# Moving one row sum (S.1) later in VectorE's order, and three last stores to other issuers, in a convolution with max pooling

## The chip, the cores and the metric

The kernel runs on one core of a Trainium2 chip. The metric is the time of one execution on the device, in microseconds, lower is better. Five engines work side by side, each through its own list of instructions in order: TensorE (PE in the profile, its weight loads PEld), VectorE (DVE), ScalarE (ACT), GpSimd (POOL) and SyncE (SP). SP issues DMA transfers only; ScalarE and GpSimd can issue them too.

## The reference

```python
x_pad = np.pad(x, ((0, 0), (0, 0), (1, 1), (1, 1)))            # x: 16 x 64 x 64 x 64, f32
for kh in range(3):
    for kw in range(3):                                        # weight: 128 x 64 x 3 x 3
        conv[b, co] += weight[co, ci, kh, kw] * x_pad[b, ci, kh:kh+64, kw:kw+64]
output[b, c, i, j] = np.max(conv[b, c, 2*i:2*i+2, 2*j:2*j+2])  # 16 x 128 x 32 x 32
```

## The kernel before

Two images lie on the 128 partitions, 64 channels each; `h` (0 or 1) is the image of the pair. The pictures are cut into quarters of 16 rows, that is 8 pooled rows, so that one product of TensorE is 64 channels by 8 rows by 64 columns and fills one of the eight PSUM banks (`acc[:, bank]`). There are 32 such units, handled in two ways. A K unit reads a bf16 copy of its rows (`kx`) and takes five products; a W unit reads f32 rows (`wx`), forms four sums of rows and takes four products. Write r0 and r1 for the two picture rows of a pooled row, r-1 and r2 for their neighbours, G0, G1, G2 for the three rows of the filter. Both kinds split the two convolved rows into a part that they share and a part of each. The maximum of the two separate parts is taken first (VectorE), TensorE then adds the shared part into the same bank, and the maximum over neighbouring columns follows.

A text, `ORDER`, holds every step of the kernel in one sequence written out by hand; each engine gets its own steps in that sequence, and semaphores between engines follow from the data. A step is a name, the unit's number and, for most, the image:

- `E.i` (VectorE) or `e.i` (GpSimd): r1 - r0 of W unit i. `S.i` (VectorE): r0 + r1 of W unit i. `Z.i` and `Y.i` (GpSimd): r-1 - r1 and r2 - r0. `KS.i` (VectorE): r0 + r1 of K unit i. All are line 260, and their tiles are called we, ws, wz, wy and ks.
- `P...` (TensorE, line 202): products, two of them joined by a plus sign and interleaved, three matmuls each (one per filter column). P2, P0, P3 and P1 of a W unit read we, wz, wy and ws; PAa, PAb, PBa and PBb of a K unit read kx, PR reads ks. P1 and PR add the shared part. A number after a colon is the bank.
- `EV`/`ev` (ScalarE, line 290): one bank copied to SBUF; `SE` (ScalarE, line 295): minus one bank into another; `MX`/`mx` (VectorE, line 299): the maximum of a bank and a copied one, written back into the bank; `OD`/`od` (ScalarE, line 303): the odd columns copied out; `CM`/`cm` (VectorE, line 327): the maximum of even and odd columns into the output tile `o`. Capitals are K units, small letters W units.
- `X...`: casts of the first K unit's rows to bf16. `LD.i`: load of a W unit's rows, issued by SP. `L<n>`: load of two K units' rows, issued by GpSimd with a cast on the way.

Two rules outside `ORDER` bear on the change. The first is an order edge: every sum that GpSimd makes waits for the VectorE step with two SBUF operands (E, S, KS and the like) that stands last before it in `ORDER`:

```python
def on_vector(inst):
    sbuf_op[0] = inst
    return inst

def on_gpsimd(inst):
    behind(inst, sbuf_op[0])
    return inst
```

The second is the way in which the last stores are issued. `act_left` counts the ScalarE steps that are still to come in `ORDER`. The outputs of the last two units are stored image by image; a store that comes up while `act_left` is 1 or 0 goes into a list, `late`, and is issued once `act_left` is 0, the first from that list by ScalarE, the second by SyncE, and so on in turn. All others are issued by SyncE at once.

The last steps of `ORDER` that matter to this are `CM.12.1 od.18.0 cm.18.0 OD.12.0 CM.12.0 od.18.1 cm.18.1`.

Of the kernel before, what the change touches and what calls it, by code (L numbers as in the profile page):

```python
# [10 lines left out]
def kernel(  # L11
# [274 lines left out]
    ev, od, ot = {}, {}, {}  # L286
# [19 lines left out]
    act_left = [0]  # L306
# [2 lines left out]

    def store_late(dst, src):  # L310
        late.append((dst, src))
        if act_left[0] <= 1:
            flush_late()

    def flush_late():
        while late and act_left[0] == 0:
            stored["late"] = stored.get("late", 0) + 1
            queue = nc.scalar if stored["late"] % 2 else nc.sync
            dst, src = late.pop(0)
            queue.dma_start(out=dst, in_=src)  # L320

    def colmax(c, i, h):
        g = (c, i, h)
        if (c, i) not in ot:
            ot[c, i] = o_pool.tile([128, 2, R, WO], FP32, name="o")
        o = ot[c, i]
        nc.vector.tensor_tensor(  # L327
            out=o[:, h],
            in0=acc[:, tb[g], :, 0::2],
            in1=od.pop(g),  # L330
            op=MAX,
        )
        free.add(tb.pop(g))
        p, q = place[c, i]
        dst = out[2 * p : 2 * p + 2, :, q * R : (q + 1) * R, :].rearrange("b c h w -> c b (h w)")
        src = o.rearrange("p b h w -> p b (h w)")
        stored[c, i] = stored.get((c, i), 0) + 1
        if order_of.index((c, i)) >= len(order_of) - 2:
            if act_left[0] <= 1:
                store_late(dst[:, h], src[:, h])  # L340
            else:
                nc.sync.dma_start(out=dst[:, h], in_=src[:, h])
        elif stored[c, i] == 2:
            nc.sync.dma_start(out=dst, in_=src)
# [72 lines left out]
    for name, f in ("ev", evac), ("mx", rowmax), ("od", odd), ("cm", colmax):  # L417
        steps[name] = lambda i, h, f=f: f("w", i, h)
        steps[name.upper()] = lambda i, h, f=f: f("k", i, h)
# [7 lines left out]
        PAx.0.0:6+PAx.0.1:7 GM/V PAa.0.0+PAa.0.1 VD0/A VG1/V LD.1 PAb.0.0+PAb.0.1 XE/V VG2/A TGM:2 KS.0  # L427
        TGP:4 E.0 VGM/A PBa.0.0:0+PBa.0.1:1 EV.0.0 Z.0 VGP/V LD.2 PBb.0.0+PBb.0.1 EV.0.1 MX.0.0
        P2.0.0:4+P2.0.1:3 X1/A S.0 X1b/A L0 PAy.1.0:7+PAy.1.1:2 PAa.1.0+PAa.1.1 SE.0.1:5 MX.0.1 Y.0 SE.0.0:6
        PAb.1.0+PAb.1.1 X2/A E.1 PR.0.0+P0.0.1 EV.1.0 P0.0.0+PR.0.1 EV.1.1 S.1 LD.3 ev.0.1 PBa.1.0:7+P3.0.1 KS.1 Z.1 OD.0.1  # L430
        P2.1.0:2+PBa.1.1:3 OD.0.0 CM.0.1 ev.0.0 mx.0.1 P3.0.0+PBb.1.1 SE.1.0:4 Y.1 PBb.1.0+P2.1.1:1 MX.1.1
        P0.1.0+P1.0.1 CM.0.0 e.2 MX.1.0 SE.1.1:0 P3.1.0+PR.1.1 LD.4 mx.0.0 ev.1.0 PR.1.0+P0.1.1 Y.2 LD.5
        OD.1.1 mx.1.0 od.0.1 P1.0.0+P3.1.1 OD.1.0 CM.1.1 ev.1.1 P1.1.0+P2.2.1:2 cm.0.1 Z.2 od.0.0 mx.1.1
        PAa.2.0:5+PAa.2.1:3 SE.2.1:1 CM.1.0 PAb.2.0+PAb.2.1 L1 od.1.0 cm.0.0 KS.3 PBa.2.0:7+PBa.2.1:6 EV.2.1
        E.3 LD.6 PBb.2.0+P0.2.1 EV.2.0 S.2 LD.7 P2.2.0:3+P1.1.1 KS.2 ev.2.1 Z.3 cm.1.0 PAa.3.0:5+PBb.2.1
# [117 lines left out]
```

## Time and profile before

| | us |
|---|---|
| median of 3 runs | 105.14 (104.82 to 105.29) |
| the profiled execution, its own time | 105.48 |
| its span in the profile | 103.6 |
| TensorE busy | 97.3 (94% of the span) |
| VectorE busy | 89.2 (86%) |
| ScalarE busy | 81.9 (79%) |
| GpSimd busy | 67.1 (65%) |
| 16 DMA engines, mean rate | 220 GB/s |

The granted TensorE clock of the profiled execution was 0.995 of full speed. The profiled execution is 0.34 us above the median, and 1.88 us of its time lie outside the span. In the views below, an instruction's line gives its start in us from the start of the span, how long it took (or how long a merged group of instructions took in all), engine, line, operation, output and inputs, and in brackets the idle time of the engine before it with the event that ended the idle time. A TensorE weight load overlaps matmuls, and an engine may start an instruction some hundredths of a microsecond before the end of the one before it.

### The profile page before, as it was taken

The page shows a single profiled execution, that of the slowest core. Times are in us where ns is not written, and L with a number is a line of the kernel's source. Part 1 is how long each engine was busy: PE and PEld are TensorE (multiplying, and loading weights), DVE is VectorE, ACT ScalarE, POOL GpSimd, SP SyncE. Part 2 cuts the span into 40 slices and gives each one's busy share as a digit, 9 for nine tenths or more (in the row PEclk, how much of TensorE's full clock was granted, in tenths as well). Part 3 has the DMA queues.
Part 4 walks back from the last instruction along what each step waited for, and adds up shares of the span by engine and source line. Part 5 has one row for each costly group of instructions (what it writes and reads, how often), then busy time and mean ns, then how long its engine had stood idle before and what let it go on. Part 6 is the DMA issues. An engine that isn't in the chain of part 4 may idle for free.

```text
span 103.6 us, 2522 instructions
## 1 busy us (share of the span) xinstructions
PE 97.3 (94%) x894; PEld 53.4 (52%) x894; DVE 89.2 (86%) x178; ACT 81.9 (79%) x178; POOL 67.1 (65%) x76
## 2 busy tenths in 40 slices
PE   6899998999999999999999999999999999999920
PEld 2365434555665555555555755555555555666600
DVE  1697598999698999987988999989999999989960
ACT  4579966887897867799879988889889988988640
POOL 7306559947959687976895946892993598590000
PEclk9999999999999999999999999999999999999997
DMA  2987988899999997589989988999956841512352
GB/s 59 354 284 224 234 196 286 237 300 165 284 382 320 161 212 291 192 201 206 218 195 327 357 224 264 299 218 222 378 190 139 197 173 41 196 70 76 131 210 96
DMA packets 13069, 22.81 MB, mean 220 GB/s; under 512 B 1024, under 2 KB 9216, under 8 KB 13056
## 3 DMA queue, kind: packets, MB, share of 16 engines
q1 hardware_dynamic: 12048, 19.63, 58.0%
q0 software_dynamic: 864, 2.88, 18.8%
q8 instruction: 7, 0.11, 0.5%
q10 hardware_dynamic: 144, 0.13, 0.4%
q14 instruction: 6, 0.05, 0.2%
HBM read 17.14 MB, written 8.39 MB: 246 GB/s over the span
## 4 chain that ended last, share of the span: by engine, by line
PE 76%; DMA 8%; DVE 8%; POOL 2%; issue 2%
PE acc L202 75%; DMA wx<-in_x_dram 6%; DMA wraw<-in_weight_dram 3%; DVE acc L299 2%; DVE o L327 2%; POOL wz L260 1%; POOL wy L260 1%; DVE wq L395 1%; DVE we L260 1%; DVE ws L260 1%; DVE wq L364 0%; DVE wq L356 0%; DVE wt L180 0%; PE acc L164 0%; DVE ks L260 0%
## 5 line engine op out<-in xcount | busy, mean ns | idle before, releaser
L202 PEld LDWEIGHTS <-wt 64*128 64x128 bf16 x858 | 50.8, 94 | 41.3 <-issue 1.2
L202 PE MATMUL acc<-kx,wt 64*128 64x512 bf16 (+4 forms) x324 | 57.1, 365 | 0.0
L299 DVE TENSOR_TENSOR acc<-acc,ev 128x512 f32<-128x512 f32 x64 | 42.4, 692 | 4.1 <-PE acc L202 2.5
L290 ACT COPY ev<-acc 128x512 f32<-128x512 f32 x64 | 36.6, 592 | 6.2 <-PE acc L202 5.7
L260 POOL TENSOR_TENSOR wz<-wx 128x512 bf16<-128x512 f32 x19 | 24.1, 1273 | 10.9 <-DVE ks L260 4.6
L202 PE MATMUL acc<-wy,wt 64*128 64x504 bf16 (+1 forms) x114 | 29.6, 377 | 0.4 <-POOL wy L260 0.4
L260 POOL TENSOR_TENSOR wy<-wx 128x512 bf16<-128x512 f32 x19 | 24.1, 1272 | 8.2 <-PE acc L202 3.1
L202 PE MATMUL acc<-wz,wt 64*128 64x504 bf16 (+1 forms) x114 | 29.2, 376 | 0.2 <-POOL wz L260 0.2
L202 PE MATMUL acc<-we,wt 64*128 64x504 bf16 (+1 forms) x114 | 29.1, 377 | 0.0
L202 PE MATMUL acc<-ws,wt 64*128 64x504 bf16 (+1 forms) x114 | 29.1, 377 | 0.0
L327 DVE TENSOR_TENSOR o<-acc,od 128x256 f32<-128x256 f32 x64 | 25.2, 417 | 2.1 <-ACT od L303 1.7
L303 ACT COPY od<-acc 128x256 f32<-128x256 f32 x64 | 23.0, 380 | 4.5 <-PE acc L202 3.7
L295 ACT ACTIVATE acc<-acc 128x512 f32<-128x512 f32 x38 | 22.1, 587 | 3.8 <-DVE o L327 2.1
L202 PE MATMUL acc<-ks,wt 64*128 64x504 bf16 (+1 forms) x78 | 20.2, 377 | 0.0
L260 POOL TENSOR_TENSOR we<-wx 128x512 bf16<-128x512 f32 x11 | 14.0, 1272 | 5.1 <-PE acc L202 3.4
L260 DVE TENSOR_TENSOR ws<-wx 128x512 bf16<-128x512 f32 x19 | 13.9, 738 | 0.0
L260 DVE TENSOR_TENSOR we<-wx 128x512 bf16<-128x512 f32 x8 | 6.0, 750 | 1.1 <-DMA wx<-in_x_dram 1.1
L260 DVE TENSOR_TENSOR ks<-kx 128x512 bf16<-128x512 bf16 x13 | 5.4, 419 | 0.1
L105 POOL DMA_DIRECT2D kx<-in_x_dram x6 | 3.5, 590 | 0.0
L487 PE MATMUL acc<-const-bfloat16-1.0 128*128 128x512 bf16 x6 | 2.7, 623 | 0.8 <-PEq L534 0.8
L356 DVE TENSOR_TENSOR wq<-wraw 128x192 bf16<-128x192 f32 x1 | 0.5, 502 | 2.4 <-DMA wraw<-in_weight_dram 2.4
L164 PE MATMUL acc<-ident,wq 128*128 128x128 bf16 x28 | 2.1, 220 | 0.5 <-DVE wq L395 0.3
(28 smaller groups left out, 17.6 us busy)
## 6 DMA issues: line engine op xcount, KB each, us to landing
out_dram<-o SPq DMA_DIRECT2D x30, 256.0 KB, 4.6
wx<-in_x_dram SPq DMA_DIRECT2D x9, 512.0 KB, 7.1
wx<-in_x_dram SPq DMA_DIRECT2D x5, 480.0 KB, 6.4
wx<-in_x_dram SPq DMA_DIRECT2D x4, 544.0 KB, 6.4
kx<-in_x_dram POOLq DMA_DIRECT2D x3, 496.0 KB, 8.0
kx<-in_x_dram POOLq DMA_DIRECT2D x2, 528.0 KB, 8.9
wx<-in_x_dram SPq DMA_DIRECT2D x1, 576.0 KB, 9.9
ksecond<-in_x_dram SPq DMA_DIRECT2D x2, 256.0 KB, 4.1
```

What stands on the lines that cost most here:

```text
L105: return nc.gpsimd.dma_start(out=ktile(i)[:, lo:hi, :], in_=rows_of(p, lo, hi))
L164: nc.tensor.transpose(turned_rows(m)[:, j, :], wq[:, BLOCKS[m] - 1 + j : BLOCKS[m] + 1 + j, :].rearrange("a b c -> a (b c)"), ident,)
L202: lambda kw=kw, o0=o0, o1=o1, c0=c0, c1=c1: nc.tensor.matmul(dst[:, i0:i1, o0:o1], wt[lo : lo + CI, m0 + kw - h, :], rows(lo, i0, i1, c0, c1),
L260: return engine.tensor_tensor(out=r, in0=t[:, f + a : f + a + 2 * R - 1 : 2, :], in1=t[:, f + b : f + b + 2 * R - 1 : 2, :], op=op,)
L290: nc.scalar.copy(out=ev[g], in_=acc[:, ta[g]])
L295: nc.scalar.mul(acc[:, t], acc[:, ta["w", i, h]], -1.0)
L299: nc.vector.tensor_tensor(out=t, in0=t, in1=ev.pop(g), op=MAX)
L303: nc.scalar.copy(out=od[g], in_=acc[:, tb[g], :, 1::2])
L327: nc.vector.tensor_tensor(out=o[:, h], in0=acc[:, tb[g], :, 0::2], in1=od.pop(g), op=MAX,)
L356: inst = engine.tensor_tensor(out=slots(D0), in0=g0, in1=g1, op=SUB)
L395: "D2", on_vector(nc.vector.tensor_sub(out=slots(D2), in0=g2, in1=g1))
L487: warm = nc.tensor.matmul(acc[:, n], src[:, 0:128], src, start=True, stop=True, skip_group_check=True)
```

## The change

S.1, which stood before KS.1 and Z.1, now stands behind MX.1.0 and just ahead of e.2. So VectorE's order is E.1, KS.1, CM.0.1, mx.0.1, MX.1.1, CM.0.0, MX.1.0, S.1, mx.0.0 in place of E.1, S.1, KS.1, CM.0.1, mx.0.1, MX.1.1, CM.0.0, MX.1.0, mx.0.0. TensorE's, ScalarE's and GpSimd's compute steps keep their order. By the order edge, Z.1 and Y.1 wait for KS.1 as before; e.2, Y.2 and Z.2, which also waited for KS.1, now wait for S.1.

The bound on `act_left` is raised from 1 to 2, so that the store of cm.18.0 also goes into the list. The stores of cm.18.0, CM.12.0 and cm.18.1 were issued by SyncE, ScalarE and SyncE; now they are issued by ScalarE, SyncE and ScalarE, after the last ScalarE copy in `ORDER`.

```diff
     def store_late(dst, src):
         late.append((dst, src))
-        if act_left[0] <= 1:
-            flush_late()
+        flush_late()
...
         if order_of.index((c, i)) >= len(order_of) - 2:
-            if act_left[0] <= 1:
+            if act_left[0] <= 2:
                 store_late(dst[:, h], src[:, h])
...
-        PAb.1.0+PAb.1.1 X2/A E.1 PR.0.0+P0.0.1 EV.1.0 P0.0.0+PR.0.1 EV.1.1 S.1 LD.3 ev.0.1 PBa.1.0:7+P3.0.1 KS.1 Z.1 OD.0.1
+        PAb.1.0+PAb.1.1 X2/A E.1 PR.0.0+P0.0.1 EV.1.0 P0.0.0+PR.0.1 EV.1.1 KS.1 Z.1 LD.3 ev.0.1 PBa.1.0:7+P3.0.1 OD.0.1
         P2.1.0:2+PBa.1.1:3 OD.0.0 CM.0.1 ev.0.0 mx.0.1 P3.0.0+PBb.1.1 SE.1.0:4 Y.1 PBb.1.0+P2.1.1:1 MX.1.1
-        P0.1.0+P1.0.1 CM.0.0 e.2 MX.1.0 SE.1.1:0 P3.1.0+PR.1.1 LD.4 mx.0.0 ev.1.0 PR.1.0+P0.1.1 Y.2 LD.5
+        P0.1.0+P1.0.1 CM.0.0 MX.1.0 S.1 e.2 SE.1.1:0 P3.1.0+PR.1.1 LD.4 mx.0.0 ev.1.0 PR.1.0+P0.1.1 Y.2 LD.5
         OD.1.1 mx.1.0 od.0.1 P1.0.0+P3.1.1 OD.1.0 CM.1.1 ev.1.1 P1.1.0+P2.2.1:2 cm.0.1 Z.2 od.0.0 mx.1.1
         PAa.2.0:5+PAa.2.1:3 SE.2.1:1 CM.1.0 PAb.2.0+PAb.2.1 L1 od.1.0 cm.0.0 KS.3 PBa.2.0:7+PBa.2.1:6 EV.2.1
         E.3 LD.6 PBb.2.0+P0.2.1 EV.2.0 S.2 LD.7 P2.2.0:3+P1.1.1 KS.2 ev.2.1 Z.3 cm.1.0 PAa.3.0:5+PBb.2.1
         od.1.1 MX.2.0 SE.2.0:2 PAb.3.0+P3.2.1 cm.1.1 Y.3 MX.2.1 PR.2.0+P2.3.1:4 EV.3.0 mx.2.1
         P0.2.0+PAa.3.1:0 OD.2.0 S.3 P2.3.0:5+P1.2.1 ev.2.0 CM.2.0 e.4 P3.2.0+PAb.3.1 od.2.1 SE.3.1:3 cm.2.1
```

## The prediction

> **What bounds the kernel now.** I read the page first, then the chain of work that ended last, then the timelines of single engines around the place that the chain points to.
>
> ```profile
> span 103.6 us, 2522 instructions
> ...
> PE 97.3 (94%) x894; PEld 53.4 (52%) x894; DVE 89.2 (86%) x178; ACT 81.9 (79%) x178; POOL 67.1 (65%) x76
> ```
> ```profile
> 12.48 0.02 issue
> 12.50 0.69 DVE we L260
> 13.20 0.60 DVE ws L260
> 13.80 0.35 DVE ks L260
> 14.14 0.07 issue
> 14.21 1.27 POOL wz L260
> 15.48 1.24 POOL wy L260
> 16.73 0.04 issue
> 16.77 77.93 PE acc L202 x718
> ```
>
> TensorE is the bound, and the chain says more: from 16.77 to 94.70 us it is TensorE alone, with no wait. Ahead of that stands a serial piece that starts when LD.1 lands (12.48): E.1, S.1, KS.1, then GpSimd's Z.1 and Y.1. A moment won there is worth its length at the end, if nothing later makes TensorE wait for it. What the piece costs TensorE is in its timeline:
>
> ```profile
> 14.99 0.38 PE L202 MATMUL acc<-we,wt 64*128 64x504 bf16 x1
> 15.54 0.37 PE L202 MATMUL acc<-wz,wt 64*128 64x512 bf16 x1 [0.16 <-POOL wz L260]
> ...
> 16.77 0.37 PE L202 MATMUL acc<-wy,wt 64*128 64x512 bf16 x1 [0.41 <-POOL wy L260]
> ```
>
> Pairs of matmuls start every 0.216 us (14.56, 14.78, 14.99), a step of three pairs takes 0.65. So wz was due at 15.21 and came 0.33 late; wy, due 0.65 after 15.54, came 0.58 late.
>
> **The front: what S.1 gives up.** S.1 holds VectorE for 0.60 us, from 13.11 to the start of KS.1 at 13.71. Without it KS.1 can start at 13.11: it needs the cast X2, which ScalarE ended at 11.63 (the row that starts at 11.01 and takes 0.62). It ends 0.42 later, 13.53. Z.1 started 0.08 after KS.1's end, so now 13.61 to 14.88; Y.1 starts 1.23 after Z.1 (15.44 - 14.21), so 14.84 to 16.11. P0.1.0+P1.0.1 runs when due, 15.21; P3.1.0+PR.1.1, due 15.86, waits for Y.1 plus the 0.05 seen before it (16.72 to 16.77) and starts at 16.16. TensorE then leads by 16.77 - 16.16 = 0.61 us.
>
> **Where S.1 goes.** It is not hidden in a gap big enough for it. MX.1.1 needs P3.0.0+PBb.1.1, whose last matmul ends at 14.72 whatever VectorE does; with the 0.09 that such a start takes (17.57 to 17.67) MX.1.1 starts at 14.82, only 0.16 before its old 14.98. From there by the distances of the old starts (0.60 after a 512-element maximum, 0.33 after a 256-element one): CM.0.0 15.41, MX.1.0 15.74, S.1 16.34 to 17.03, mx.0.0 16.94 to 17.64 (before: 16.51 to 17.20). P1.0.0+P3.1.1 would be due at 16.16 + 1.30 = 17.46 but needs mx.0.0: 17.67, a lead of 0.39 on the old 18.06.
>
> e.2 now waits for S.1: 17.03 + 0.08 = 17.11, after GpSimd has stood idle since 16.11. Before it started at 16.67. It takes 1.27 and is read by P2.2.1, old start 18.73, new start 18.38 + 0.05 = 18.43: the lead is 0.30. S.1's own reader, P1.1.0 (18.71), has it in time. Behind e.2 on GpSimd stand Y.2, Z.2 and the load L1, all now 0.44 late: Z.2 ends at 20.85 and L1 is issued at 20.79. P0.2.1 wants Z.2 at 21.30 - 0.30 = 21.00, so it is still in time. On SP, the stores of CM.0.0 and cm.0.0's units and LD.4 to LD.7 move up by 0.2 to 0.3 us with the steps that release them; LD.3 hangs on E.1 and stays.
>
> **What the delayed GpSimd meets.** The VectorE steps that follow are mx.1.0 17.54, CM.1.1 18.15, cm.0.1 18.48, mx.1.1 18.81, CM.1.0 19.42, cm.0.0 19.75, KS.3 20.08. Before, KS.3 started at 20.42, just after Z.2's end (19.14 + 1.27 = 20.41). Now Z.2 runs on for 0.77 us after KS.3's turn. What that costs is in the trace, in other places:
>
> ```profile
> 75.61 1.28 POOL L260 TENSOR_TENSOR wy<-wx 128x512 bf16<-128x512 f32 x1
> 76.85 1.28 POOL L260 TENSOR_TENSOR wz<-wx 128x512 bf16<-128x512 f32 x1
> ```
> ```profile
> 77.48 1.19 DVE L260 TENSOR_TENSOR we<-wx 128x512 bf16<-128x512 f32 x1
> 78.59 0.68 DVE L260 TENSOR_TENSOR ws<-wx 128x512 bf16<-128x512 f32 x1
> ```
> ```profile
> 63.31 0.45 DVE L260 TENSOR_TENSOR ks<-kx 128x512 bf16<-128x512 bf16 x1
> ```
>
> The we at 77.48 begins with 0.64 of GpSimd's wz to go and takes 1.19 in place of 0.68; GpSimd's op keeps its length. The overlap less 0.13 is lost, and the sum ends 0.55 after GpSimd's. The ks at 63.31 agrees: 0.17 of overlap with a wy that ends at 63.48, 0.45 in place of 0.42, end 0.28 after GpSimd's. So KS.3 ends at 20.85 + 0.28 = 21.13 and E.3 starts, 0.08 before that end, at 21.05; before, 20.75. VectorE is now 0.30 behind its old times while TensorE is 0.30 ahead of its own.
>
> The Trainium skill, page "SBUF — State Buffer", section "SBUF: two separate sides", gives the reason and a harder price: a VectorE operation with two SBUF inputs and a GpSimd operation contend for one port pair under an exclusive lock, held for the whole instruction by whichever started first. By its letter KS.3 would begin only at 20.85, E.3 would be 0.44 late, and the total below would come out 0.14 us higher, 105.21; the rows above, where 0.13 is hidden, decide for me.
>
> ```profile
> 21.96 0.42 DVE L260 TENSOR_TENSOR ks<-kx 128x512 bf16<-128x512 bf16 x1
> ...
> 23.58 1.29 DVE L299 TENSOR_TENSOR acc<-acc,ev 128x512 f32<-128x512 f32 x2
> ...
> 26.46 0.42 DVE L327 TENSOR_TENSOR o<-acc,od 128x256 f32<-128x256 f32 x1 [0.61 <-ACT od L303]
> ```
>
> VectorE has no idle time to make this up before 26.46. E.3, S.2, KS.2, cm.1.0, MX.2.0, cm.1.1, MX.2.1 and mx.2.1 follow back to back. mx.2.1 ended at 24.86 and P1.2.1 began at 25.21; at 24.86 + 0.30 + 0.05 = 25.21 it begins where it did. The lead is spent: 0.61, 0.39, 0.30, 0.00. Bounds for the last figure: if the collision cost nothing, 0.30 would remain; if nothing of KS.3's 0.42 lay under Z.2, TensorE would stand 0.14 behind its old time. I take 0.00, by the rows of the same two operations.
>
> After that: the idle 0.61 before 26.46 takes up VectorE's 0.30. GpSimd stays 0.30 late through e.4, Z.4 and Y.4 (end 29.33, now 29.63), so E.5, at 29.36, starts 0.27 before that end and loses 0.14; MX.3.1 then ends 0.14 late, at 31.46, and its reader PR.3.1 starts at 31.60. Nothing more is lost.
>
> **The tail.**
>
> ```profile
> 99.14 0.92 SPq L342 DMA_DIRECT2D out_dram<-o  x2
> 99.74 0.37 ACTq L320 DMA_DIRECT2D out_dram<-o  x1
> 100.15 0.41 SPq L320 DMA_DIRECT2D out_dram<-o  x1
> ```
>
> The last store (cm.18.1, data ready at 100.05) is issued at 100.15, 0.09 after SP has done with the store before it (100.06); it lands 2.2 us later, and the end follows. With ScalarE as its issuer, the queue is free: cm.18.0's store can go out when cm.18.0 is ready (99.38) and takes 0.37, CM.12.0's goes to SP at 99.74 as it did to ScalarE. The last is then issued at about 100.08. Gain 0.07; bounds 0 (an issue by ScalarE behind its own last copy, 99.59 + 0.37, and 0.1 of queue) and 0.09.
>
> **The sum.** Front 0.00, tail -0.07. The profiled execution took 105.48 (span 103.6 and 1.88 around it), which gives 105.41; it stands 0.34 above the median of the runs shown, and the same 0.07 off 105.14 gives 105.07.
>
> **The rivals.**
> - The lead survives. For it: TensorE is the only engine on the chain for 78 us, and the 0.61 at 16.77 is plain. Against: e.2's new wait and the 0.77 us under which KS.3 falls. If S.1 and the collision cost nothing, 0.61 + 0.07 gives 104.46; if only the collision costs nothing, 0.30 + 0.07 gives 104.77.
> - Slower, by the load L1. Behind e.2 it is issued 0.44 later, and behind LD.6 and LD.7 rather than ahead of them. Before, it took from 20.35 to 29.19 and PAa.5.1 first read it at 30.32, so 1.1 us of cover, 0.7 after the delay. Such loads took 5.1 to 10.3 us to land (median 8.4). At 10.3 it lands at 31.1, TensorE waits 0.8, and the time is 105.14 + 0.8 - 0.07 = 105.87. It decides from a landing later than 9.5 us after issue. Against it: the five comparable loads have one over 9.1.
> - The change does nothing on the chip: no chance, since VectorE's list and e.2's wait do change.
>
> **How the numbers follow.** 0.5% here is 0.53 us, about what a measurement of this kernel can tell from no change (its three runs spread by 0.47). The lead spent, 105.07, with its own range 104.85 to 105.3: 0.60. Lead kept in part, 104.77: 0.10. Lead kept whole, 104.46: 0.16. L1 late, 105.87: 0.14. The first has a little beyond 0.53 on each side (0.03 each, for delays between engines that the trace of one execution doesn't fix). So faster 0.19, slower 0.17, same 0.64. The range 104.45 to 105.5 leaves out L1's case and those tails.
>
> **What would show it.** In the changed trace: Z.1 at 13.6 and wy's first matmul at 16.16 (the front); VectorE's ws between two maxima at 16.3 and GpSimd's we at 17.1 (the wait); a ks at about 20.1 of some 1.05 us in place of 0.42 (the collision); the first ws matmul of P1.2.1 at 25.2 (the lead spent); a last store of ScalarE at 100.1. I am wrong if that ks keeps 0.42 us, if TensorE is still ahead at 26 us, or if it shows a wait for L1 near 30 us.

## The result, and the profile after

| | before | after |
|---|---|---|
| median, beside each other on the same chip | 105.08 us (104.79 to 105.49, 11 runs) | 105.86 us (105.09 to 106.64, 11 runs) |
| ratio after / before | | 1.0079 (95% interval 1.0050 to 1.0109) |
| profiled execution: time, span | 105.48, 103.6 | 105.27, 103.4 |

The changed kernel is 0.8% slower: 0.36 us beyond the range, on the side that had a chance of 0.17. Its runs are also spread evenly over 1.55 us where those of before stay within 0.70, and the one that was profiled is among the quickest. So its profile shows the steps of the change, but not the loss of the median run. In the tables below, medians and ranges are of all runs, but the ratios leave out a run over 1.5% above the quickest of its kernel; one run of before with KS.3 moved, at a granted clock of 0.66, took 150.58 us and is left out of its range too.

The page of the changed kernel, its span and busy times:

```profile
span 103.4 us, 2523 instructions
...
PE 97.7 (94%) x894; PEld 68.4 (66%) x894; DVE 89.9 (87%) x178; ACT 81.2 (79%) x178; POOL 67.1 (65%) x76
```

Its chain of work that ended last, from 8 us on (start, length, what):

```profile
8.02 7.95 PE acc L202 x78
15.97 0.01 issue
15.98 0.36 PE acc L202
16.34 0.59 DVE ws L260
16.93 0.62 DVE acc L299
17.55 0.04 issue
17.59 79.15 PE acc L202 x730
```

The serial piece of the kernel before (E.1, S.1, KS.1, Z.1, Y.1) is no longer on the chain: wy's first matmul starts at 15.98 instead of 16.77. In its place stands S.1, called ws here, and behind it mx.0.0, for which TensorE waits until 17.59 (18.06 before). Then the steps as predicted, in VectorE's and in GpSimd's timeline:

```profile
16.24 0.68 DVE L260 TENSOR_TENSOR ws<-wx 128x512 bf16<-128x512 f32 x1
16.84 1.29 DVE L299 TENSOR_TENSOR acc<-acc,ev 128x512 f32<-128x512 f32 x2
...
19.96 1.06 DVE L260 TENSOR_TENSOR ks<-kx 128x512 bf16<-128x512 bf16 x1
20.94 0.68 DVE L260 TENSOR_TENSOR we<-wx 128x512 bf16<-128x512 f32 x1
```
```profile
17.00 1.27 POOL L260 TENSOR_TENSOR we<-wx 128x512 bf16<-128x512 f32 x1 [1.08 <-DVE ws L260]
18.24 1.27 POOL L260 TENSOR_TENSOR wy<-wx 128x512 bf16<-128x512 f32 x1
19.46 1.27 POOL L260 TENSOR_TENSOR wz<-wx 128x512 bf16<-128x512 f32 x1
20.67 0.57 POOL L105 DMA_DIRECT2D kx<-in_x_dram  x1
```

GpSimd stands idle for 1.08 us ahead of e.2, which waits for S.1; KS.3 falls under Z.2 and takes 1.06. The last line is the issue of the load L1. Where it stands among SP's transfers turned out to matter most. SP's timeline around it, first of the kernel after, then of the kernel before, and GpSimd's issue of L1 in the kernel before:

```profile
19.74 0.91 SPq L343 DMA_DIRECT2D out_dram<-o  x2
20.70 1.30 SPq L113 DMA_DIRECT2D wx<-in_x_dram  x2
```
```profile
20.20 0.91 SPq L344 DMA_DIRECT2D out_dram<-o  x2
21.16 0.98 SPq L113 DMA_DIRECT2D wx<-in_x_dram  x2
```
```profile
20.35 0.57 POOL L105 DMA_DIRECT2D kx<-in_x_dram  x1
```

Before: first store 20.20, L1 20.35, second store 20.69, LD.6 21.16. After: both stores (19.74 and 20.24), then L1 at 20.67 and LD.6 at 20.70. The stores are those of K unit 1 and W unit 0, 256 KB each. They moved up with VectorE's maxima, while L1 moved back with e.2, Y.2 and Z.2.

At 25 us TensorE's timeline, first after, then before, shows whether the lead is spent. P2.3.0 (we) and P1.2.1 (ws) are interleaved here:

```profile
24.85 0.38 PE L202 MATMUL acc<-we,wt 64*128 64x512 bf16 x1
25.08 0.37 PE L202 MATMUL acc<-ws,wt 64*128 64x512 bf16 x1
```
```profile
25.19 0.38 PE L202 MATMUL acc<-we,wt 64*128 64x512 bf16 x1
25.21 0.38 PE L202 MATMUL acc<-ws,wt 64*128 64x512 bf16 x1
```

P1.2.1 waits for mx.2.1 and starts 0.13 ahead of its old time, P2.3.0 starts 0.34 ahead. The next step begins at 25.53 (25.84 before), so P1.2.1's wait of some 0.2 costs the other product of the pair only 0.03. TensorE is still ahead of the first profile of before, by 0.31 in one product of the pair and by 0.13 in the other.

### The profile page after: what moved, and what is told of

It reads as the page before. It is cut to its first block, busy times and chain, and to the rows that moved or that the text cites. A ratio compares the mean times of both kernels' runs of the same rounds, so it can differ in the third digit from the quotient of the medians.

```text
span 103.4 us, 2523 instructions
## 1 busy us (share of the span) xinstructions
PE 97.7 (94%) x894; PEld 68.4 (66%) x894; DVE 89.9 (87%) x178; ACT 81.2 (79%) x178; POOL 67.1 (65%) x76
## 4 chain that ended last, share of the span: by engine, by line
PE 87%; DVE 5%; DMA 3%; issue 1%
PE acc L202 86%; DMA wraw<-in_weight_dram 3%; PE acc L164 2%; DVE acc L299 1%; DVE o L326 1%; DVE wq L394 1%; DVE ws L260 1%; DVE wq L355 0%
## 5 line engine op out<-in xcount | busy, mean ns | idle before, releaser
L202 PEld LDWEIGHTS <-wt 64*128 64x128 bf16 x858 | 65.8, 94 | 26.0 <-issue 1.7
L202 PE MATMUL acc<-kx,wt 64*128 64x512 bf16 (+3 forms) x324 | 57.7, 365 | 0.0
L260 DVE TENSOR_TENSOR ks<-kx 128x512 bf16<-128x512 bf16 x13 | 6.1, 467 | 0.1
L164 PEld LDWEIGHTS <-wq 128*128 128x128 bf16 x28 | 1.6, 97 | 1.8 <-issue 0.9
```

Source lines behind the costliest of these rows:

```text
L164: nc.tensor.transpose(turned_rows(m)[:, j, :], wq[:, BLOCKS[m] - 1 + j : BLOCKS[m] + 1 + j, :].rearrange("a b c -> a (b c)"), ident,)
L202: lambda kw=kw, o0=o0, o1=o1, c0=c0, c1=c1: nc.tensor.matmul(dst[:, i0:i1, o0:o1], wt[lo : lo + CI, m0 + kw - h, :], rows(lo, i0, i1, c0, c1),
L260: return engine.tensor_tensor(out=r, in0=t[:, f + a : f + a + 2 * R - 1 : 2, :], in1=t[:, f + b : f + b + 2 * R - 1 : 2, :], op=op,)
```

## The experiments

### Which part of the change costs

The change once more; S.1's move alone, with the stores at the end as before; the last stores alone, with S.1 in its old place:

```diff
 s1_only, against the change
-        flush_late()
+        if act_left[0] <= 1:
+            flush_late()
...
-            if act_left[0] <= 2:
+            if act_left[0] <= 1:
 stores_only, against the kernel before
-        if act_left[0] <= 1:
-            flush_late()
+        flush_late()
...
-            if act_left[0] <= 1:
+            if act_left[0] <= 2:
```

> The changed kernel as it is. Eleven executions of it lie between 105.09 and 106.64 us, where the kernel before lies between 104.79 and 105.49: the change adds a spread, not a fixed step. Theory 1 (the load L1): L1 is issued late behind e.2 and is only just there when TensorE first reads it near 30.0 us (29.86 in the profiled execution, 0.15 us of cover); in an execution of over 105.8 us the profile shows L1 landing after 30.0 and TensorE waiting for it there. Theory 2 (the port): the late GpSimd sums block VectorE by more in the slow executions, and TensorE waits for maxima between 23 and 32 us, with L1 in time. Theory 3 (the stores): the end of the span after the last VectorE operation grows from 3.5 us.

> S.1 behind MX.1.0 as in the change, the last stores as before. Theories 1 and 2: as slow and as spread as the whole change, 105.9 plus 0.1 (105.2 to 106.7). Theory 3: as before, 105.1, spread 0.5.

> The last three stores issued by ScalarE, SyncE, ScalarE as in the change, S.1 in its old place. Theories 1 and 2: 0.07 us less than before, 105.0, with the old spread of about 0.5. Theory 3: 105.8 with a wide spread.

| | median (range, runs) | ratio to before (95%) |
|---|---|---|
| the change again | 106.01 (105.45 to 107.67, 11) | 1.0081 (1.0048 to 1.0114) |
| S.1 alone | 106.25 (105.14 to 106.86, 9) | 1.0108 (1.0074 to 1.0142) |
| last stores alone | 105.22 (104.68 to 105.56, 12) | 0.9999 (0.9975 to 1.0024) |

The move of S.1 is the whole loss, and the new issuers of the last stores can't be told from nothing. The profile taken of the change here (its second, 105.80 us) does not show the late L1 that the first theory asks for: L1 landed at 29.89, in time, and the loss came near 60 us (the last section has it).

### L1 put far ahead: a test that misled

In the change, L1 was moved in front of e.2 in GpSimd's list:

```diff
-        P0.1.0+P1.0.1 CM.0.0 MX.1.0 S.1 e.2 SE.1.1:0 P3.1.0+PR.1.1 LD.4 ...
+        P0.1.0+P1.0.1 CM.0.0 MX.1.0 S.1 L1 e.2 SE.1.1:0 P3.1.0+PR.1.1 LD.4 ...
...
-        ... PAb.2.0+PAb.2.1 L1 od.1.0 cm.0.0 KS.3 ...
+        ... PAb.2.0+PAb.2.1 od.1.0 cm.0.0 KS.3 ...
```

> The changed kernel with the load L1 put ahead of e.2 in GpSimd's list, where GpSimd stands idle from 16.1 to 17.1 us: it is issued near 16.1 in place of 20.7. Nothing else moves. Theory 1: the slow executions go away, 104.8 to 105.1 at the median with a spread of about 0.5. Theory 2: still 105.8 with a spread of 1.5. Theory 3: the same 105.8.

106.00 us (105.67 to 106.31, 6 runs), ratio 1.0092 (1.0060 to 1.0125). I took this as the end of the theory that L1 is late. It was not: L1 was issued at 16.25 and landed at 25.19, so TensorE did not wait for it, but LD.4, issued behind it, now landed at 26.87 (22.85 in the change), and e.4 waited for that. GpSimd's timeline:

```profile
27.00 1.27 POOL L260 TENSOR_TENSOR we<-wx 128x512 bf16<-128x512 f32 x1 [1.19 <-DMA wx<-in_x_dram]
28.23 1.28 POOL L260 TENSOR_TENSOR wz<-wx 128x512 bf16<-128x512 f32 x1
29.46 1.27 POOL L260 TENSOR_TENSOR wy<-wx 128x512 bf16<-128x512 f32 x1
```

Y.4, 1.23 later than in the change (28.23), lay over E.5, and P1.3.0 started at 33.20 instead of 31.98. Not all of these 1.22 us are LD.4's: in this execution the transposes at the start were slow (last section) and P1.0.0 was 0.67 late already, so 0.55 were added behind it. Still, all six runs took over 105.6 us. One late load had been exchanged for another, so this test could not clear L1.

### Is it S.1's place on VectorE, or the blocked KS.3?

Four kernels: the kernel before a second time; the change without S.1; the change with KS.3 moved behind Z.3, out from under Z.2; and that same move in the kernel before as a control.

```diff
 no_s1
-        return taps(a, h, GP, step1(row["ws", i], 0))
+        return taps(a, h, GP, step1(row["ws", 0 if i == 1 else i], 0))
...
-        P0.1.0+P1.0.1 CM.0.0 MX.1.0 S.1 e.2 ...
+        P0.1.0+P1.0.1 CM.0.0 MX.1.0 e.2 ...
 change_ks3_moved, before_ks3_moved
-        ... L1 od.1.0 cm.0.0 KS.3 PBa.2.0:7+PBa.2.1:6 EV.2.1
-        ... KS.2 ev.2.1 Z.3 cm.1.0 PAa.3.0:5+PBb.2.1
+        ... L1 od.1.0 cm.0.0 cm.1.0 PBa.2.0:7+PBa.2.1:6 EV.2.1
+        ... KS.2 ev.2.1 Z.3 KS.3 PAa.3.0:5+PBb.2.1
```

> The unchanged kernel before, profiled a second time. The theory now (A): the front of its first profiled execution was unusual, because LD.1 landed at 12.48 there and at 11.2 to 12.3 in the five profiles since. With a landing near 11.6, E.1 should end at about 12.65 (it lies under Y.0 on GpSimd), S.1 and KS.1 follow, Z.1 starts near 13.7, and P3.1.0+PR.1.1 near 16.2 instead of 16.77, with S.1 in its old place; the span is then about 103.1 and the time about 104.9. The rival (B), by which the prediction's baseline was right and the loss comes later: P3.1.0 at 16.6 to 16.8 again and 105.3 to 105.5.

> The change with S.1 left out altogether: P1.1.0 and P1.1.1 read unit 0's ws, and e.2 waits for KS.1 only, so unit 1's products with ws are left out of the result in favour of unit 0's. Theory A (the new place of S.1 holds up MX.1.0's successor mx.0.0 and, through e.2, Y.2 and Z.2, so that KS.3 and later sums fall under GpSimd's): with S.1 gone, P1.0.0 starts near 17.1, KS.3 keeps about 0.42 us, and the time is 104.3 to 104.8, below the kernel before. Theory B (the loss comes from transfers that land late near 60 us, whatever the front does): 105.6 to 106.0, as the change.

> The change, with cm.1.0 in KS.3's place and KS.3 behind Z.3, so that KS.3 no longer starts under Z.2; S.1 stays in its new place. Theory A with the collision of KS.3 as the loss: KS.3 takes 0.42 us, MX.2.0 is early again, and the time is 105.1 to 105.5. Theory A with the delay of mx.0.0 and e.2 as the loss, the collision being only a part: 105.5 to 105.9. Theory B: 105.9 as the change.

> The same edit on the kernel before, as the control: there KS.3 started just after Z.2 had ended, so moving it has nothing to win. All theories: 104.9 to 105.3; above 105.4 would say that the edit itself costs, and its result with the change would have to be read against that.

| | median (range, runs) | ratio to before (95%) |
|---|---|---|
| change without S.1 | 104.45 (104.33 to 104.64, 4) | 0.9939 (0.9915 to 0.9963) |
| change, KS.3 moved | 106.29 (105.52 to 106.94, 8) | 1.0102 (1.0063 to 1.0142) |
| before, KS.3 moved | 104.99 (104.75 to 105.90, 9 of 10 runs) | 0.9994 (0.9967 to 1.0022) |

Without S.1 the whole lead lasts: P3.1.0 at 16.07, P1.0.0 at 17.36, and 0.70 ahead of the first profile of before from there to the end. But moving KS.3 did not help, although it did all that it should: KS.3 took 0.42, and TensorE kept a steady lead of 0.39 from 17 to 30 us. Then the profile of that kernel (106.63 us) showed the real loss. Its chain of work:

```profile
17.09 1.27 POOL we L260
18.36 0.47 POOL wy L260
18.84 0.72 issue
19.56 1.22 POOL wz L260
20.77 10.70 DMA kx<-in_x_dram
31.48 0.05 issue
31.52 66.65 PE acc L202 x611
```

L1 took 10.70 us, 8.84 in the first profile of before, and TensorE waits for it until 31.52. That is the prediction's own slower rival. The second profile of the kernel before told nothing on its question: the 16 transposes of TensorE near 5 us took 1.79 us instead of 1.07, so its front was late for another reason (P3.1.0 at 16.98, 106.05 us).

### L1 alone made late, in the kernel before

S.1 and everything else in their old places; L1 only waits for KS.3, or for E.3 (then it stands behind E.3 in `ORDER`, just ahead of LD.6):

```diff
+        if n == 1:
+            behind(inst, mark["KS3"])        # before_l1_e3: mark["E3"]
...
-        ... PAb.2.0+PAb.2.1 L1 od.1.0 cm.0.0 KS.3 PBa.2.0:7+PBa.2.1:6 EV.2.1
+        ... PAb.2.0+PAb.2.1 od.1.0 cm.0.0 KS.3 L1 PBa.2.0:7+PBa.2.1:6 EV.2.1
```

> The smaller dose: the kernel before with L1 behind KS.3, issued at about 20.9 and still some 0.2 ahead of LD.6. Theory L: L1 lands at 30 to 31, and the time is 105.1 to 105.9, between the kernel before and the larger dose. Theory A: 105.0 to 105.4.

> The kernel before, S.1 in its old place, with nothing changed but L1, which waits for E.3 and so is issued at about 21.4 instead of 20.4, just behind LD.6. Theory L: L1 lands at 31 to 32, TensorE waits for it by 0.7 to 1.7, and the time is 105.7 to 106.9. Theory A: 105.0 to 105.4, since every VectorE and GpSimd step keeps its place.

The smaller dose: 106.48 us (106.21 to 108.90, 4 runs), ratio 1.0122 (1.0078 to 1.0167). The larger: 106.64 (106.48 to 107.07, 4 runs), 1.0144 (1.0108 to 1.0180). The smaller one costs more than expected. It puts L1 (20.60) behind both stores (19.66 and 20.15) and beside LD.6 (20.62), which is where the change puts it. Its chain of work:

```profile
18.64 1.22 POOL wz L260
19.86 0.73 issue
20.59 0.01 POOLq L260
20.60 10.46 DMA kx<-in_x_dram
31.06 0.04 issue
31.11 66.65 PE acc L202 x611
```

Up to L1's landing TensorE was 0.54 ahead of the first profile of before; behind P1.3.0 it was 0.85 late. So L1's later issue alone, in the smaller dose some 0.7 us behind Z.2's end (19.88) and past the second store, makes a loss of the change's kind and more.

### What makes it late: LD.6 behind it, or the stores ahead?

First LD.6 (with LD.7 behind it) was held until E.3 had ended, in the change and in the change with KS.3 moved:

```diff
-        behind(wload(i), mark.get({0: "D2", 1: "GM", 2: "E0", 3: "E1"}.get(i)))
+        behind(wload(i), mark.get({0: "D2", 1: "GM", 2: "E0", 3: "E1", 6: "E3"}.get(i)))
```

> The change, with LD.6 (and LD.7 behind it) held until E.3 has ended, so that L1 starts about 0.9 us ahead of LD.6 as it does in the kernel before, and not in the same moment. Theory L (the loss is L1: issued 0.3 later and beside LD.6, it lands anywhere from 29.6 to 31.5, and TensorE needs it at about 30.0): L1 lands at 29.0 to 30.1 in the profile, and the time is 105.0 to 105.3, with the runs closer together than the change's 105.1 to 106.6. Theory A (the loss is in VectorE's order: mx.0.0, e.2 and the blocked sums): 105.7 to 106.1 and as wide as the change.

> Both edits on the change: KS.3 behind Z.3, and LD.6 held until E.3 has ended. Theory L: without the load's wait, TensorE keeps the lead of about 0.4 that it showed with KS.3 moved until 30 us, and the time is 104.8 to 105.1. Theory A: 105.7 to 106.3, as with KS.3 moved alone.

No help: 106.07 us (105.31 to 107.14, 10 runs), ratio 1.0075 (1.0048 to 1.0103), and 106.82 (105.46 to 107.40, 10 runs), 1.0113 (1.0071 to 1.0154). In both profiles L1, issued at 20.6, had 0.6 to 1.0 us of start on LD.6 and still landed at 32.0 only.

Then the two stores. One kernel leaves them out; the others hold the second one (W unit 0) until E.3 has ended, so that the issues come in the old order: store, L1, store, LD.6.

```diff
 change_no_stores
-        elif stored[c, i] == 2:
+        elif stored[c, i] == 2 and (c, i) not in (("k", 1), ("w", 0)):
 change_store_late, change_ks3_store, before_store_late
         elif stored[c, i] == 2:
-            nc.sync.dma_start(out=dst, in_=src)
+            if (c, i) == ("w", 0):
+                held.append((dst, src))
+            else:
+                nc.sync.dma_start(out=dst, in_=src)
...
         mark[f"E{i}"] = inst
+        if i == 3 and held:
+            dst, src = held.pop()
+            behind(nc.sync.dma_start(out=dst, in_=src), inst)
```

> The change without the two stores that SP issues just ahead of L1 (the outputs of K unit 1 and W unit 0, 512 KB, which this kernel leaves unwritten). L1 and LD.6 still start at 20.7. If L1's late landing is what the change lost: L1 lands at 27 to 29, no wait near 30 us, 104.9 to 105.2 with runs within 0.6 us of each other. If the loss is elsewhere: 105.6 to 106.1.

> The change with the second of these stores (W unit 0) held until E.3 has ended, so that the order of issue is again that of the kernel before: store, L1, store, LD.6, LD.7. If it is L1's place behind the second store and beside LD.6 that makes it late: L1 lands at 28.4 to 30.1 and the time is 105.0 to 105.3. If L1 is late because it is issued at 20.7 when TensorE runs ahead, whatever stands around it: 105.5 to 106.1, as with LD.6 held.

> The same held store on the change with KS.3 behind Z.3. If the order of issue is the cause: TensorE keeps its lead of 0.4 to 0.5 from 20 us on, and the time is 104.8 to 105.1. If not: 106.0 to 106.8, as before this edit, since TensorE then needs L1 0.15 earlier still.

> The same held store on the kernel before, as the control. There L1 already starts ahead of that store: 104.9 to 105.3 by either.

| | median (range, runs) | ratio to before (95%) |
|---|---|---|
| change, both stores left out | 105.30 (104.78 to 106.07, 10) | 1.0007 (0.9974 to 1.0040) |
| change, second store held | 105.20 (105.11 to 105.60, 10) | 1.0009 (0.9982 to 1.0036) |
| the same, KS.3 moved too | 105.18 (104.87 to 105.75, 10) | 1.0014 (0.9991 to 1.0037) |
| before, second store held | 104.97 (104.83 to 105.52, 10) | 0.9996 (0.9973 to 1.0020) |

Holding one store of 256 KB back takes the loss away and draws the runs together to 0.49 us, with S.1 in its new place and L1 issued at 20.71 as in the change. In its chain of work TensorE has no wait between 17.63 and 94.59; SP's timeline shows the new order around L1's 20.71:

```profile
17.63 76.96 PE acc L202 x704
```
```profile
19.78 0.40 SPq L350 DMA_DIRECT2D out_dram<-o  x1
21.68 0.39 SPq L281 DMA_DIRECT2D out_dram<-o  x1
22.12 1.46 SPq L113 DMA_DIRECT2D wx<-in_x_dram  x2
```

Three limits. SP issues in order, so LD.6 and LD.7 are held with the store (LD.6 at 22.12, 21.58 with LD.6 held by itself); I take the store for the cause because holding LD.6 alone did nothing. And leaving the stores out let LD.6 start at 17.89, long ahead of L1, so that its 105.30 with a wide spread supports this less cleanly than the held store does. And the one profile of the change with the held store does not show a quicker L1: it took 9.39 us and landed at 30.10, later than in the first profile of the change (29.86), so that KS.4 started 0.1 late. That the store's place shortens L1's time to land rests on the run times, on the pair with KS.3 moved (10.70 without the held store, 8.74 with it) and on the means below. None of these beats the kernel before by more than the measurement can tell.

### The change itself, profiled twice more

> The change itself, profiled once more, to see the wait in the change and not only in its relatives. Theory L: the execution's time goes with L1's landing. Landed by 30.1, 105.1 to 105.4 (unless a load near 60 us is late as well); landed at 30.5 to 32, TensorE stops near 30 us for the difference and the time is 105.6 to 107.

> The same again, since L1's landing differs from one execution to the next: the same relation of landing, wait and time.

105.92 and 105.95 us, and both wait for L1. (The first also began with slow transposes, and its P1.0.0 is 0.4 late.) Its chain of work, then VectorE's timeline, are:

```profile
16.75 0.59 DVE ws L260
17.34 0.62 DVE acc L299
17.96 0.04 issue
18.00 12.79 PE acc L202 x113
30.79 0.02 issue
30.82 66.65 PE acc L202 x611
```
```profile
29.64 0.83 DVE L260 TENSOR_TENSOR we<-wx 128x512 bf16<-128x512 f32 x1
30.80 0.43 DVE L260 TENSOR_TENSOR ks<-kx 128x512 bf16<-128x512 bf16 x1 [0.33 <-DMA kx<-in_x_dram]
31.14 0.42 DVE L326 TENSOR_TENSOR o<-acc,od 128x256 f32<-128x256 f32 x1
31.47 1.29 DVE L299 TENSOR_TENSOR acc<-acc,ev 128x512 f32<-128x512 f32 x2
```

L1 landed at 30.77, and two engines were waiting: VectorE with KS.4 and TensorE with PAa.5.1. KS.4, cm.2.0, MX.3.1 and mx.3.0 follow back to back, and P1.3.0 needs the last of them. The profiles that tell most:

| kernel | L1 issued | landed | took | P1.3.0 starts | behind the landing | time |
|---|---|---|---|---|---|---|
| L1 ahead of the second store: | | | | | | |
| before | 20.35 | 29.19 | 8.84 | 32.24 | 3.05 | 105.48 |
| before, second store held | 19.81 | 28.64 | 8.84 | 31.71 | 3.07 | 104.91 |
| change without S.1 | 19.65 | 28.14 | 8.49 | 31.55 | 3.41 | 104.64 |
| change, second store held | 20.71 | 30.10 | 9.39 | 32.14 | 2.04 | 105.23 |
| L1 behind both stores: | | | | | | |
| change, first profile | 20.67 | 29.86 | 9.18 | 31.98 | 2.13 | 105.27 |
| change, second profile (LD.12 late too) | 20.62 | 29.89 | 9.27 | 31.93 | 2.04 | 105.80 |
| change, fourth profile | 20.64 | 30.50 | 9.86 | 32.54 | 2.04 | 105.95 |
| change, third profile | 21.09 | 30.77 | 9.68 | 32.81 | 2.04 | 105.92 |
| before, L1 behind KS.3 | 20.60 | 31.06 | 10.46 | 33.10 | 2.04 | 106.21 |
| before, L1 behind E.3 | 21.28 | 31.34 | 10.06 | 33.38 | 2.04 | 106.48 |
| change, KS.3 moved | 20.77 | 31.48 | 10.70 | 33.52 | 2.04 | 106.63 |
| change, LD.6 held | 20.61 | 32.00 | 11.38 | 34.04 | 2.04 | 107.14 |

Wherever L1 lands too late for KS.4's turn near 30 us, P1.3.0 starts 2.04 us after the landing; the time follows, 73.1 to 73.4 us behind P1.3.0 (73.9 in the second profile of the change). The seven profiles with L1 ahead of the second store had 7.90 to 9.45 us for it (mean 8.8), the ten with L1 behind both stores 9.04 to 11.38 (mean 10.1). The ranges overlap, and the five of the ten in which only S.1's move put it there have 9.04 to 9.86 (mean 9.4).

## Why the prediction was wrong

**What held.** The steps up to 21 us, to 0.2 us or better: wy at 16.16 predicted and 15.98 found, S.1 16.34 and 16.24, P1.0.0 17.67 and 17.59, e.2 17.11 and 17.00, KS.3 at 20.08 for 1.05 and at 19.96 for 1.06. wy is 0.18 earlier because LD.1 landed at 12.29 instead of 12.48. The others are 0.08 to 0.12 earlier for another reason, since S.1 starts at 16.16 to 16.21 in executions in which LD.1 lands anywhere from 11.16 to 12.29: MX.1.1, from which they are counted, started at 14.71 and not at 14.82. The rows' price for the blocked sum was the right one: KS.3 ended 0.28 after Z.2. The last store went out 0.03 after its data instead of 0.10, the 0.07 of the tail, too little to be measured.

**The step that failed** is the one that priced L1, in the slower rival: "from 20.35 to 29.19 and PAa.5.1 first read it at 30.32, so 1.1 us of cover, 0.7 after the delay". On it L1 was left out of the sum. Three of its terms were off.
- L1's time to land was carried over as 8.84 with a 0.44 delay, which gives 29.63. Behind both stores it took 9.0 to 11.4. The prediction noticed that L1 is issued later and that SP's stores move up by 0.2 to 0.3 (0.46 in the trace); it costed each by itself and did not see that together they reverse the order of L1 and a store. It looked for the new neighbour among the loads ("behind LD.6 and LD.7"), and holding LD.6 changed nothing.
- The first reader is KS.4 on VectorE, at 29.96 before, not PAa.5.1 at 30.32: 0.77 of cover, not 1.1. Through mx.3.0 it adds some 0.25 at P1.3.0 to TensorE's own wait.
- So a delay of 0.3 in that profile, and an extra 0.2 to 2.5 us of flight, met a cover of 0.8. With these terms the rival would have had the largest chance and not 0.14. Its mechanism was right. That its time, 105.87, is the measured 105.86 is luck in part: it had the wait as 0.8 on top of an unchanged time, while the third and the fourth profile show 0.45 and 0.62 (2.39 and 2.56 us from P3.3.0 to P1.3.0, 1.94 before).

**The lead at 25 us**, "0.61, 0.39, 0.30, 0.00", did not end at 0.00 either, and the sign "TensorE is still ahead at 26 us" came up: 0.31 in one product of the pair, 0.13 in the other. VectorE was 0.19 behind its old times and not 0.30 (E.3 at 20.94), and the sum took P1.2.1's start for that of the whole step. This lead is one over the first profile of before only, as follows.

**The baseline** was off as well. "The lead 0.61" was measured from an execution in which LD.1 landed at 12.48, later than in any of the others (11.16 to 12.38). With S.1 in its old place and LD.1 at 11.75 to 11.90 (the held store in the kernel before, the smaller dose) P1.0.0 starts at 17.52, and so it does in the change (17.51 to 17.63 wherever TensorE's start was not late). So the lead over an ordinary execution of before is nothing at P1.0.0, since mx.0.0 behind S.1 is then the last to be ready, and about 0.25 is lost by 30 us to sums that fall under GpSimd's, KS.3 above all (-0.29 in the change, -0.54 in before with the store held). Moving KS.3 too brought back 0.18 of it. Such an execution of before also issues L1 at 19.81, so that the change issues it 0.8 later and not 0.3. And holding the store does not make the two kernels alike: none of its ten runs is below 105.11 us, where twelve of thirty of before beside it are below 105.0. The change then seems to even out a late LD.1 at the price of the quickest runs, though no single run shows both.

**The account.** The change costs 0.78 us (105.08 to 105.86). With one store held it costs 0.07 (ratio 1.0009, interval 0.9982 to 1.0036). So some 0.7 go with the order of L1 and that store, and what is left can't be told from nothing, nor from the predicted -0.07. By what these 0.7 act is shown in part: two of the three slower profiled executions of the change wait for L1, by 0.45 and 0.62, and the third lost its time to LD.12; how often each happens in the unprofiled runs is not shown. What the DMA engines do with L1's packets behind the stores, and why its landing differs by 2 us between executions of the same order, is open. The Trainium skill, page "DMA: Bandwidth & Descriptors", section "Issuing engines are not separate DMA queues", says that transfers issued by SP and by GpSimd run on the same 16 engines and interleave there; the runs agree as far as they go, since holding back a store of SP takes away a loss that goes with a load of GpSimd.

## What to carry to other kernels

When an edit moves work between engines, write down the order in which the DMAs around it are issued, before and after, for all issuers together: a load that slipped behind a 256 KB store took 10.1 us here in place of 8.8 (means of ranges that overlap), and its cover ends at its first reader on any engine. A single profiled execution says how late the loads were in that execution only; take a lead from the loads' usual landing, and take a widened spread of the runs as a hint that a transfer's landing may have come onto the path. An experiment that moves a load far ahead tests the load that it overtakes as well.

## What the runs showed of the hardware

The same load in the same place lands at different times: LD.1 between 11.16 and 12.48 us, 4.5 to 5.9 after its issue. LD.12, issued at 50.5 to 51.5 in the unhindered executions, landed at 58.1 to 60.9, 7.3 to 9.4 after its issue, and when it comes late it costs more: in the change's second profile (105.80 us) Z.12 starts at 60.86, S.11 on VectorE falls under it and takes 1.63 us, 0.68 when nothing stands in its way. VectorE's and GpSimd's timelines:

```profile
61.05 1.63 DVE L260 TENSOR_TENSOR ws<-wx 128x512 bf16<-128x512 f32 x1
```
```profile
60.86 1.27 POOL L260 TENSOR_TENSOR wz<-wx 128x512 bf16<-128x512 f32 x1 [1.55 <-DVE acc L299]
```

The row puts GpSimd's wait down to a maximum of VectorE, but in six profiles, with LD.12 landing at 59.80 to 60.86, Z.12 starts 0.16 after that landing each time, here after 60.70. TensorE lost 0.76 there, so the wait for L1 is not the only loss of single executions. The kernel before had it too, in its second profile (LD.12 at 60.86).

The 16 transposes near 5 us took 1.07 or 1.08 us in thirteen of nineteen profiled executions and 1.32, 1.44 and 1.75 to 1.85 in the other six; the trace's record of the full clock begins at 3.5 to 5.2 us in the thirteen, and at 5.5, 5.9 and 6.5 to 6.6 in those. Where it is late, TensorE's front is up to 0.7 later, and both kernels pass that on (P1.0.0 at 18.2 to 18.3 with 1.75 to 1.85, at 17.5 to 17.6 with 1.07 and LD.1 in time). The Trainium skill, page "TensorE: Matmul & The Clock Gate", section "Part 1: The HAM clock gate (the "warmup" mystery)", says that the clock's window runs free of the program, so that the length of the cold part varies between runs of one kernel; these times agree that it varies.
